# Queries first, keys last and two gate cells at the end of layer 1's first projections

## The chip, the core and the metric

The kernel runs on one core of a Trainium2 chip. Its engines are TensorE (PE in the profile; PEld is its weight load), VectorE (DVE), ScalarE (ACT), GpSimd (POOL) and SyncE (SP), each with an instruction queue of its own that it works off in order. Transfers between the chip's memory (HBM) and SBUF are issued on the queues of SP, ACT and POOL and carried by 16 DMA engines. The metric is the time of one execution on the device in microseconds (us): 3739.16 as the median of three runs, from 3738.85 to 3740.12.

## What is computed

Two layers of a diffusion backbone over 2048 latent tokens and 256 context tokens, width 1024, all in float32. Layer 0 is latent attention beside gated linear attention, layer 1 neighbourhood attention on a 32 by 64 grid. What matters here is the input projection of layer 1:

```
q, k, v, z = jnp.split(dot(h, w_in), 4, axis=-1)          # 16 heads of 64 each
q, k = rms_norm(heads(q), q_gain), rms_norm(heads(k), k_gain)
o = neighborhood_attention(q, k, v, k_ctx, v_ctx, rpb)
y = dot(o * silu(z), w_out)
```

Keys and values are wanted for all 2304 tokens, queries and the gate `z` for the latent ones only.

## The kernel before

Tokens lie in 18 row tiles of 128; tiles 0 and 1 are context. The columns of `w_in` lie in eight blocks of 512, numbered `j`: 0 and 1 queries, 2 and 3 keys, 4 and 5 values, 6 and 7 the gate. One **cell** (t, j) is the product of row tile t with column block j. Every float32 operand is split in a high and a low part, and the product is the sum of three (lines 129 to 131), so a cell is 24 matmuls of 128x512 into one PSUM bank (`gm`).

The projections stand in two functions. `odd_qk` runs the query and key cells and, at its end, the first two value cells (16, 4) and (17, 4). `odd_vz` runs the other value cells and the gate cells, from the last tile down, and weaves between them the scores `mx` whose block maxima (`maxes`) the attention needs later.

Only four column blocks of the weight have room at a time, in places `w0` to `w3`. Block 4 takes the place of block 2, 5 that of 3, 6 that of 0, 7 that of 1 (`OD_PLACE`). When the last cell of a block is issued, `done` hands its successor to `self.ahead`, and `pump` issues it piece by piece. A piece, here called a chunk, is 128x512 numbers, 256 KB: a load on SP (line 380, tile `wraw`, three in flight), ScalarE's copy as the high part and VectorE's difference as the low part (line 383). A load waits until the chunk three before it is split.

A query or key cell ends on ScalarE with squares (`osq`), on VectorE with sums (line 1135), on GpSimd with the power that makes the norm (lines 200 and 202), on VectorE with the scaled tile `onat` (line 1138). `fin` follows two cells later: four transposes into the bank `tp` (line 1146), then scaled copies. A query tile makes `oqh` and `oql`, stored to `Q1` by SP (line 1158). A key tile makes `oqh`, stored to `K1` by SP (line 1151), and its part of the grid-ordered `okt`; after every fourth latent tile `store_k` sends four stores of 512 KB to `K1t` on POOL (line 1179). A value cell only copies the bank (`onat` or `ovz`) and stores it to `V1` on POOL (line 1201). A gate cell takes a tanh on ScalarE, one product on VectorE (line 1227) that makes `z (1 + tanh(z/2))`, four transposes (line 1230), a copy `ozt` and a store to `z1` on ACT's queue (line 1234).

`cells` runs the first two and the last two tiles in pairs: before the change the last eight cells of `odd_qk`'s main list are keys (16, 2), (17, 2), (16, 3), (17, 3), then queries (16, 0), (17, 0), (16, 1), (17, 1).

The order in each engine's queue is not that of the source: a scheduler sets it when the kernel is built, by its own estimates of time. The pools of `odd_vz` take over the memory of `odd_qk`'s, and a tile of the new pool waits only for what lay in its bytes. VectorE clears the buffers `mz` (line 1239) and `mm` (line 1252) first, so it waits there for the stores that still read that memory. The loads of `mk` from `K1` (line 1246), of the bias table `mtab` (line 1248) and of `mq` from `Q1` (line 1258) wait on SP in the same way.

Of the kernel before, what the change touches and what calls it, by code (L numbers as in the profile page):

```python
# [10 lines left out]
F32 = mybir.dt.float32  # L11
F32R = mybir.dt.float32r
AF = mybir.ActivationFunctionType
ALU = mybir.AluOpType
# [3 lines left out]
P = 128  # L18
D = 1024
KD = D // P  # L20
SEQ = 2048
CTX = 256
T = SEQ + CTX
NT = T // P
NCT = CTX // P
# [63 lines left out]
class Kern:  # L89
# [1011 lines left out]
    def odd_qk(self, ws, win, hT):  # L1101
        nc = self.nc
        self.V1c = self.scr("V1c", (2, P, NCT, 512), F32)
        self.V1 = self.scr("V1", (2, SEQ, 512), F32)
        self.Q1 = self.scr("Q1", (2, 8, P, SEQ), F32)
        self.K1 = self.scr("K1", (8, P, T), F32)
        self.K1t = self.scr("K1t", (8, 2, P, T), F32)
        with ExitStack() as es:
            sp = self.pool(es, "osA", bufs=2, side="left", reuse_waits="tile")
            pp = self.pool(es, "opA", bufs=2, space=PSUM, reuse_waits="tile")  # L1110
            qkg = self.tl(sp, [P, 2], "oqkg", bufs=1)
            nc.sync.dma_start(qkg[:], self.i["od_gain"])
            nc.vector.tensor_scalar(out=qkg[:, 0:1], in0=qkg[:, 0:1], scalar1=0.125, scalar2=None, op0=ALU.mult)
            self.ahead += [self.od_steps(win, 0, ws), self.od_steps(win, 1, ws)]
            pend, kt = [], {}

            def cell(t, j):
                hi, lo = hT[t]
                wh, wl = win[j]
                ps = self.tl(pp, [P, 8, 64], "gm", bufs=3)  # L1120
                steps = self.mm3_steps(ps[:], (lambda k: hi[:, k, :], lambda k: lo[:, k, :]),
                                       (lambda k: wh[:, k, :], lambda k: wl[:, k, :]), range(KD))
                for n, _ in enumerate(steps):
                    if n == 5 and pend and (len(pend) > 1 or j == 4):
                        fin(*pend.pop(0))
                    yield
                if j == 4:
                    n = self.tl(sp, [P, 512], "onat", bufs=4)
                    self.act(n[:], ps[:].rearrange("p h d -> p (h d)"))
                    self.store_v(t, 0, n)  # L1130
                    return
                sq = self.tl(sp, [P, 512], "osq")
                self.act(sq[:], ps[:].rearrange("p h d -> p (h d)"), AF.Square)
                ss = self.tl(sp, [P, 8], "oss", bufs=4)
                nc.vector.tensor_reduce(out=ss[:], in_=sq[:].rearrange("p (h d) -> p h d", h=8), axis=AX.X, op=ALU.add)
                self.rpow(ss[:], ss[:], 1.0 / 64, EPS)
                n = self.tl(sp, [P, 512], "onat", bufs=4)
                nc.vector.tensor_tensor(out=n[:].rearrange("p (h d) -> p h d", h=8), in0=ps[:],
                                        in1=ss[:].unsqueeze(2).to_broadcast([P, 8, 64]), op=ALU.mult)
                pend.append((t, j, n))  # L1140

            def fin(t, j, n):
                z = j // 2
                ps = self.tl(pp, [P, 4, P], "tp")
                for i in range(4):
                    nc.tensor.transpose(ps[:, i, :], n[:, i * P : i * P + P], self.ident[:])
                hi = self.tl(sp, [P, 4, P], "oqh", F32R)
                self.act(hi[:], ps[:], AF.Copy, scale=qkg[:, z : z + 1])
                j0 = (j % 2) * 4
                if z == 1:  # L1150
                    nc.sync.dma_start(self.K1[j0 : j0 + 4, :, t * P : t * P + P].rearrange("j p t -> p j t"), hi[:].bitcast(F32))
                if z == 0 or t < NCT:
                    lo = self.tl(sp, [P, 4, P], "oql", F32R)
                    nc.vector.scalar_tensor_tensor(out=lo[:], in0=ps[:], scalar=qkg[:, z : z + 1], in1=hi[:],
                                                   op0=ALU.mult, op1=ALU.subtract)
                    if z == 0:
                        for part, tt in enumerate((hi, lo)):
                            nc.sync.dma_start(self.Q1[part][j0 : j0 + 4, :, (t - NCT) * P : (t - NCT) * P + P].rearrange("j p t -> p j t"),
                                              tt[:].bitcast(F32))
                    else:  # L1160
                        store_k((hi, lo), j0, t * P, P)
                    return
                g, r0 = divmod(2 * (t - NCT), 8)
                if r0 == 0:
                    kt[j] = [self.tl(sp, [P, 4, 512], f"okt{j}{part}", F32R, bufs=1) for part in range(2)]
                view = lambda x, n: x[:].rearrange("p i (r c b) -> p i r c b", r=n, c=4)
                for r in range(2):
                    oh, ol = (x[:].rearrange("p i (c b r) -> p i r c b", c=4, r=8)[:, :, r0 + r] for x in kt[j])
                    self.act(oh, view(ps, 2)[:, :, r], AF.Copy, scale=qkg[:, z : z + 1])
                    nc.vector.scalar_tensor_tensor(out=ol, in0=view(ps, 2)[:, :, r], scalar=qkg[:, z : z + 1],  # L1170
                                                   in1=view(hi, 2)[:, :, r], op0=ALU.mult, op1=ALU.subtract)
                if r0 == 6:
                    store_k(kt.pop(j), j0, CTX + g * 512, 512)

            def store_k(parts, j0, o, w):

                for u, x in enumerate(parts):
                    for i in range(2):
                        nc.gpsimd.dma_start(self.K1t[j0 : j0 + 4, i, u * 64 : u * 64 + 64, o : o + w].rearrange("j d t -> d j t"),
                                            x[i * 64 : i * 64 + 64].bitcast(F32))  # L1180

            nxt = {2: 4, 3: 5, 0: 6, 1: 7}
            done = lambda j: j in nxt and self.ahead.append(self.od_steps(win, nxt[j], ws))
            cells = self.cells(list(range(NT)), (2, 3, 0, 1), lambda t, j: j > 1 or t >= NCT) + [(NT - 2, 4), (NT - 1, 4)]
            for _ in self.stream(cells, hT, cell, lambda t: self.prep(1, t, self.x1, pp, ("px", 2)), done):
                self.pump()
            while pend:
                fin(*pend.pop(0))

    def by_tile(self, out, in_):  # L1190

        self.act(out.rearrange("d (c r b) -> d r c b", c=4, r=8), in_.rearrange("d (r c b) -> d r c b", r=8, c=4))
# [9 lines left out]

    def odd_vz(self, ws, win, hT):
        nc = self.nc
        self.z1 = self.scr("z1", (KD, P, SEQ), F32)
        self.M1 = self.scr("M1", (16, SEQ), F32)
        NR, NC = (len(b) for b in BLOCKS["q"])
        with ExitStack() as es:
# [6 lines left out]
            def cell(t, j):  # L1215
                hi, lo = hT[t]
                wh, wl = win[j]
                ps = self.tl(pp, [P, 512], "gm")
                yield from self.mm3_steps(ps[:], (lambda k: hi[:, k, :], lambda k: lo[:, k, :]),
                                          (lambda k: wh[:, k, :], lambda k: wl[:, k, :]), range(KD))  # L1220
                n = self.tl(sp, [P, 512], "ovz", bufs=3)
                if j < 6:
                    self.act(n[:], ps[:])
                    self.store_v(t, j - 4, n)
                    return
                self.last_tanh = self.act(n[:], ps[:], AF.Tanh, scale=0.5)
                nc.vector.scalar_tensor_tensor(out=n[:], in0=n[:], scalar=1.0, in1=ps[:], op0=ALU.add, op1=ALU.mult)
                pt = self.tl(pp, [P, 4, P], "tp", bufs=1)
                for i in range(4):
                    nc.tensor.transpose(pt[:, i, :], n[:, i * P : i * P + P], self.ident[:])  # L1230
                z = self.tl(sp, [P, 4, P], "ozt", bufs=1)
                self.act(z[:], pt[:])
                o = (t - NCT) * P
                nc.scalar.dma_start(self.z1[(j - 6) * 4 : (j - 6) * 4 + 4, :, o : o + P].rearrange("j p t -> p j t"), z[:])
# [53 lines left out]
                        nc.gpsimd.dma_start(self.M1[h, g * 512 : g * 512 + 512].rearrange("(a c b) -> c a b", a=8, c=4),  # L1288
                                            r[4 * g : 4 * g + 4].rearrange("c (a b) -> c a b", a=8).bitcast(F32))

            cells = self.cells(list(range(NT))[::-1], (4, 5, 6, 7), lambda t, j: (j > 4 or t < NT - 2) and (j < 6 or t >= NCT))
            gemms = self.stream(cells, hT, cell, lambda t: self.reload(1, t))
            self.weave(gemms, maxes(), 0.57, 15)

# [388 lines left out]
```

## Time and profile before

| | |
|---|---|
| median of three runs | 3739.16 us (3738.85 to 3740.12) |
| the profiled execution, whole | 3741.73 us |
| its span, first to last instruction | 3739.6 us |
| `odd_qk` about | 2188 to 2635 us |
| `odd_vz` about | 2635 to 3105 us |

A row of the timeline has the start in us, the duration, the engine, the source line, the operation and its tiles, output before `<-`; in brackets stands how long the engine had been idle before it and what released it. `x2` means that two equal instructions are merged. A line of the waits says who waited for whom, then the total, the count and the longest. In the table by stretches the columns are the stretch, its length, the busy time of PE, PEld, DVE, ACT and POOL with counts, the granted clock of TensorE, the mean busy share of the DMA engines and GB/s.

### The profile page before, as it was taken

How to read it: one execution, taken by the hardware profiler on the slowest of the kernel's cores; microseconds unless marked ns; L12 is line 12 of the kernel's file. 1: busy time of each engine (PE TensorE's matmuls, PEld its weight loads, DVE VectorE, ACT ScalarE, POOL GpSimd, SP SyncE). 2: the span in 40 equal slices, each digit the busy share in tenths (PEclk: the TensorE clock that was granted, in tenths of full speed). 3: DMA queues.
4: the chain of work that ended last, by engine and by line, in shares of the span. 5: the costliest groups of instructions: out<-in, count | busy, mean ns of one | idle time of the engine just before them, and what ended most of it. 6: DMA issues, size and time to landing. Idle time of an engine off the chain costs nothing.

```text
span 3739.6 us, 51736 instructions
## 1 busy us (share of the span) xinstructions
PE 3583.3 (96%) x18404; PEld 2768.3 (74%) x18404; DVE 2379.7 (64%) x4860; ACT 1437.7 (38%) x2741; POOL 1207.2 (32%) x1334
## 2 busy tenths in 40 slices
PE   8999989999999999999999999999899998898889
PEld 6988988888886666655657878887788885555567
DVE  4677656888866666697654344545678774666722
ACT  4445541111125555545552134444322223454400
POOL 1434330001011222212202233333344435776643
PEclk9999999999999999999999999999999998999899
DMA  7455462222252241434515545546544448777464
GB/s 254 137 165 160 128 172 94 84 75 86 74 137 66 69 114 56 115 88 137 142 51 169 165 148 149 146 142 182 183 141 143 130 116 223 186 182 201 141 194 132
DMA packets 365267, 512.18 MB, mean 137 GB/s; under 512 B 25825, under 2 KB 244913, under 8 KB 359106
## 3 DMA queue, kind: packets, MB, share of 16 engines
q1 hardware_dynamic: 322642, 425.49, 39.7%
q0 software_dynamic: 19712, 55.40, 4.9%
q10 hardware_dynamic: 22656, 27.99, 2.1%
q8 instruction: 146, 2.39, 0.3%
q14 instruction: 111, 0.91, 0.1%
HBM read 329.38 MB, written 179.37 MB: 136 GB/s over the span
## 4 chain that ended last, share of the span: by engine, by line
PE 79%; DVE 7%; DMA 6%; POOL 3%; ACT 3%; issue 2%; SPq 0%; POOLq 0%; DVEq 0%; ACTq 0%
PE gm L129 9%; PE gm L130 9%; PE gm L131 9%; PE av L905 7%; PE st L963 4%; PE mx L651 4%; PE st L964 3%; PE st L965 3%; PE pj L129 3%; PE pj L131 3%; PE pj L130 3%; DMA wraw<-w_od 2%; PE o L1393 2%; PE st L1363 2%; PE o L1375 1%
## 5 line engine op out<-in xcount | busy, mean ns | idle before, releaser
L954 DVE TENSOR_TENSOR acc<-acc,apt 128x512 f32<-128x512 f32 x512 | 364.5, 736 | 156.6 <-ACT apt L106 153.6
L106 ACT ACTIVATE apt<-st 128x512 f32<-128x512 f32 (+1 forms) x592 | 343.9, 593 | 283.9 <-PE st L965 246.5
L652 DVE TENSOR_REDUCE mm<-mx 128x1 f32<-128x512 f32 (+1 forms) x656 | 389.1, 628 | 82.2 <-PE mx L651 75.2
L905 PE MATMUL av<-apt,av 128*64 128x512 f32 (+1 forms) x1184 | 286.2, 597 | 0.0
L963 PE MATMUL st<-aq,akh 97*128 97x512 f32 (+1 forms) x592 | 254.1, 429 | 5.9 <-ACT apt L106 3.0
L1399 POOL TENSOR_TENSOR oacc<-oacc,opt 128x576 f32<-128x576 f32 (+6 forms) x192 | 221.4, 1179 | 86.6 <-ACT opt L106 84.9
L651 PE MATMUL mx<-mk,mq 96*128 96x512 f32 (+1 forms) x656 | 236.8, 373 | 5.8 <-DMA mq<-QT 4.6
L964 PE MATMUL st<-aq,akh 96*128 96x512 f32 (+1 forms) x592 | 235.1, 397 | 0.0
L965 PE MATMUL st<-aq,akl 96*128 96x512 f32 (+1 forms) x592 | 233.9, 396 | 0.0
L1277 DVE CUSTOM_DVE_ANT_1 mx<-mx,mtab 128x225 f32<-128x225 f32 (+13 forms) x576 | 183.6, 339 | 57.8 <-PE mx L1271 42.6
L106 ACT ACTIVATE u<-gm 128x352 f32<-128x352 f32 (+1 forms) x140 | 68.5, 497 | 369.5 <-PE gm L131 208.8
L905 PEld LDWEIGHTS av<-apt,av 128*64 128x64 f32 x1184 | 81.6, 137 | 155.4 <-issue 154.1
L1521 DVE TENSOR_TENSOR opt<-st,tab 128x64 f32<-128x64 f32 (+10 forms) x576 | 142.4, 315 | 79.9 <-PE st L1364 52.7
L963 PEld LDWEIGHTS st<-aq,akh 97*128 97x128 f32 x592 | 112.4, 190 | 99.0 <-issue 43.7
L1073 POOL TENSOR_TENSOR px<-py,px 128x512 f32<-128x512 f32 x64 | 86.3, 1349 | 234.3 <-DVE py L1072 223.0
L106 ACT ACTIVATE opt<-opt 128x930 f32<-128x930 f32 (+8 forms) x130 | 104.4, 805 | 138.9 <-DVE opt L1521 130.1
L1363 PE MATMUL st<-q,kt 128*128 128x480 f32 (+5 forms) x256 | 104.3, 409 | 47.7 <-DVE opt L1521 43.4
L651 PEld LDWEIGHTS mx<-mk,mq 96*128 96x128 f32 x656 | 121.7, 189 | 17.3 <-issue 5.0
L106 ACT ACTIVATE prh<-pr 128x1024 fp32r<-128x1024 f32 x32 | 33.8, 1057 | 261.6 <-PE pj L130 234.0
L965 PEld LDWEIGHTS st<-aq,akl 96*128 96x128 f32 x592 | 113.6, 192 | 25.6
L964 PEld LDWEIGHTS st<-aq,akh 96*128 96x128 f32 x592 | 114.1, 193 | 18.0
L129 PE MATMUL gm<-w1h,hhi 128*128 128x512 f32 x288 | 116.4, 404 | 6.0 <-ACT onat L106 6.0
(511 smaller groups left out, 10033.2 us busy)
## 6 DMA issues: line engine op xcount, KB each, us to landing
q<-Q SPq DMA_DIRECT2D x48, 512.0 KB
H<-x ACTq DMA_DIRECT2D x36, 512.0 KB
adaw<-ada_w SPq DMA_DIRECT2D x64, 256.0 KB
x<-H SPq DMA_DIRECT2D x32, 512.0 KB
pr<-RT SPq DMA_DIRECT2D x32, 512.0 KB
wraw<-w_od SPq DMA_DIRECT2D x64, 256.0 KB
K1t<-okt POOLq DMA_DIRECT2D x32, 512.0 KB, 7.4
kt<-K1t SPq DMA_DIRECT2D x32, 512.0 KB
```

The lines of the kernel that those rows point to most:

```text
L106: return self.nc.scalar.activation(out, in_, func, **kw)
L129: self.nc.tensor.matmul(out, lh(k), rh(k), start=j == 0, stop=False)
L130: self.nc.tensor.matmul(out, lh(k), rl(k), start=False, stop=False)
L131: yield self.nc.tensor.matmul(out, ll(k), rh(k), start=False, stop=j == n - 1)
L651: mm = nc.tensor.matmul(ps[:, :w], q[:A_QK, (t % 6) * P : (t % 6) * P + P], k[:A_QK, k0 : k0 + w], start=True, stop=True)
L652: nc.vector.tensor_reduce(out=m[:, t, n : n + 1], in_=ps[:, :w], axis=AX.X, op=ALU.max)
L905: nc.tensor.matmul(O[j, nb][i * 64 : i * 64 + 64, :w], V[j, kt // TT][:, kt % TT, i * 64 : i * 64 + 64], pts[i][:, :w], start=n == 0, stop ...
L954: nc.vector.tensor_tensor(out=acc[i][:, :w], in0=a[:, :w], in1=pts[i][:, :w], op=ALU.add)
L963: nc.tensor.matmul(ps[:, :w], kh[: A_QK + 1, i, kq], qh[: A_QK + 1, :w], start=True, stop=False)
L964: nc.tensor.matmul(ps[:, :w], kh[:A_QK, i, kq], ql[:A_QK, :w], start=False, stop=False)
L965: mm = nc.tensor.matmul(ps[:, :w], kl[:A_QK, i, kq], qh[:A_QK, :w], start=False, stop=True)
L1399: self.psum = nc.gpsimd.tensor_tensor(out=a, in0=a, in1=pts[:, :, a0 - r0 : a1 - r0, :], op=ALU.add)
```

## The change

The last eight cells of `odd_qk` become queries first, keys last, and the two cells at the end are the first half of the gate, block 6, in place of values. Since a block's successor is loaded when the block is through, weight 6 comes first, then 7, 4 and 5. The gate's tanh and product go into a helper, and in `odd_qk` the gate tile goes through `fin` like a query or key tile; its transposed copy takes an `oqh` buffer and is stored to `z1` on POOL's queue. `pend` is drained one by one in the cells of block 6; the two gate tiles themselves are finished after the last cell. `odd_vz` begins with the other gate half and then runs the values of tiles 17 and 16, (17, 7), (16, 7), (17, 4), (16, 4), (17, 5), (16, 5); before it began with (17, 5), (16, 5), (17, 6), (16, 6), (17, 7), (16, 7). From tile 15 down it is as before.

```diff
-                    if n == 5 and pend and (len(pend) > 1 or j == 4):
+                    if n == 5 and pend and (len(pend) > 1 or j == 6):
                         fin(*pend.pop(0))
                     yield
-                if j == 4:
+                if j == 6:
                     n = self.tl(sp, [P, 512], "onat", bufs=4)
-                    self.act(n[:], ps[:].rearrange("p h d -> p (h d)"))
-                    self.store_v(t, 0, n)
+                    self.gate(n, ps[:].rearrange("p h d -> p (h d)"))
+                    pend.append((t, j, n))
                     return
...
                 hi = self.tl(sp, [P, 4, P], "oqh", F32R)
+                if j == 6:
+                    self.act(hi[:].bitcast(F32), ps[:])
+                    nc.gpsimd.dma_start(self.z1[:4, :, (t - NCT) * P : (t - NCT) * P + P].rearrange("j p t -> p j t"), hi[:].bitcast(F32))
+                    return
...
-            cells = self.cells(list(range(NT)), (2, 3, 0, 1), lambda t, j: j > 1 or t >= NCT) + [(NT - 2, 4), (NT - 1, 4)]
+            cells = self.cells(list(range(NT)), (2, 3, 0, 1), lambda t, j: j > 1 or t >= NCT)[:-8]
+            cells += [(t, j) for j in (0, 1, 2, 3, 6) for t in (NT - 2, NT - 1)]
...
+    def gate(self, out, in_):
+
+        self.last_tanh = self.act(out[:], in_, AF.Tanh, scale=0.5)
+        self.nc.vector.scalar_tensor_tensor(out=out[:], in0=out[:], scalar=1.0, in1=in_, op0=ALU.add, op1=ALU.mult)
...
-            cells = self.cells(list(range(NT))[::-1], (4, 5, 6, 7), lambda t, j: (j > 4 or t < NT - 2) and (j < 6 or t >= NCT))
+            cells = [(t, j) for j in (7, 4, 5) for t in (NT - 1, NT - 2)]
+            cells += self.cells(list(range(NT))[::-1], (4, 5, 6, 7), lambda t, j: j < 6 or t >= NCT)[8:]
```

More of the change, by code (lines that the diff above doesn't have):

```diff
@@ L1105, in odd_qk @@
         self.Q1 = self.scr("Q1", (2, 8, P, SEQ), F32)
+        self.z1 = self.scr("z1", (KD, P, SEQ), F32)
         self.K1 = self.scr("K1", (8, P, T), F32)
@@ L1204, in odd_vz @@
         nc = self.nc
-        self.z1 = self.scr("z1", (KD, P, SEQ), F32)
         self.M1 = self.scr("M1", (16, SEQ), F32)
@@ L1225, in cell @@
                     return
-                self.last_tanh = self.act(n[:], ps[:], AF.Tanh, scale=0.5)
-                nc.vector.scalar_tensor_tensor(out=n[:], in0=n[:], scalar=1.0, in1=ps[:], op0=ALU.add, op1=ALU.mult)
+                self.gate(n, ps[:])
                 pt = self.tl(pp, [P, 4, P], "tp", bufs=1)
```

## The prediction

> **What bounds the kernel now.** The page first: TensorE is busy for 96% of the span, so a change counts only where it alters TensorE's idle time or its clock.
>
> ```profile
> span 3739.6 us, 51736 instructions
> PE 3583.3 (96%) x18404; PEld 2768.3 (74%) x18404; DVE 2379.7 (64%) x4860; ACT 1437.7 (38%) x2741; POOL 1207.2 (32%) x1334
> ```
>
> Then TensorE's waits between 2540 and 2720 us, where `odd_qk` hands over to `odd_vz` (total, times, longest), and its timeline there.
>
> ```profile
> PE gm L129 <- ACT onat L106: 6.0, 1, 6.0
> PE tp L1146 <- DVE onat L1138: 2.0, 1, 2.0
> PE tp L1230 <- DVE ovz L1227: 0.7, 2, 0.5
> ...
> 2582.85 0.60 ACT L106 ACTIVATE osq<-gm 128x512 f32<-128x512 f32 x1 [9.52 <-PE gm L131]
> 2613.05 0.40 PE L131 MATMUL gm<-w3h,hlo 128*128 128x512 f32 x1
> 2627.58 0.60 PE L1146 MATMUL tp<-ident,onat 128*128 128x128 f32 x4
> 2627.94 0.48 PE L129 MATMUL gm<-w0h,hhi 128*128 128x512 f32 x1
> 2629.17 0.40 PE L131 MATMUL gm<-w0h,hlo 128*128 128x512 f32 x1
> 2635.52 0.79 PE L129 MATMUL gm<-w1h,hhi 128*128 128x512 f32 x1 [5.95 <-ACT onat L106]
> 2639.43 0.39 PE L129 MATMUL gm<-w1h,hhi 128*128 128x512 f32 x1
> ```
>
> The reader is to see one place: the last value cell ends at 2629.5, and the first cell of `odd_vz` starts at 2635.5, because its PSUM bank is freed by ScalarE's copy of the last value tile. Why is that copy late? ScalarE runs its queue in order, and weight splits stand ahead of it.
>
> ```profile
> L106 ACT ACTIVATE w0h<-wraw x8: 622/632/662, 2583.3 to 2592.7; 128x512 fp32r<-128x512 f32 x8
> L106 ACT ACTIVATE w2h<-wraw x8: 629/632/635, 2617.3 to 2634.4; 128x512 fp32r<-128x512 f32 x8
> ...
> 2587.56 1.24 ACT L106 ACTIVATE w0h<-wraw 128x512 fp32r<-128x512 f32 x2
> 2593.22 0.77 ACT L106 ACTIVATE okt<-tp,oqkg 128x256 fp32r<-128x256 f32 x1
> 2594.40 0.63 ACT L106 ACTIVATE w1h<-wraw 128x512 fp32r<-128x512 f32 x1 [0.41 <-DMA wraw<-w_od]
> 2596.58 0.63 ACT L106 ACTIVATE w1h<-wraw 128x512 fp32r<-128x512 f32 x1 [1.55 <-DMA wraw<-w_od]
> 2605.85 0.67 ACT L106 ACTIVATE oqh<-tp,oqkg 128x512 fp32r<-128x512 f32 x1
> 2606.42 0.76 ACT L106 ACTIVATE okt<-tp,oqkg 128x256 fp32r<-128x256 f32 x1
> 2609.70 1.27 ACT L106 ACTIVATE w1h<-wraw 128x512 fp32r<-128x512 f32 x2 [0.97 <-DMA wraw<-w_od]
> 2625.14 1.28 ACT L106 ACTIVATE w2h<-wraw 128x512 fp32r<-128x512 f32 x2 [0.78 <-DMA wraw<-w_od]
> 2634.36 0.63 ACT L106 ACTIVATE w2h<-wraw 128x512 fp32r<-128x512 f32 x1 [0.53 <-DMA wraw<-w_od]
> 2634.89 0.58 ACT L106 ACTIVATE onat<-gm 128x512 f32<-128x512 f32 x1
> 2657.89 1.28 ACT L106 ACT_TABLE_LOAD   x1
> ```
>
> Four weights of eight 256 KB chunks each are replaced here, 32 chunks numbered in order: 4 and 5 at 2587.56, 8 at 2592.7, 9 at 2594.40, 10 at 2596.58, 14 and 15 at 2609.70, 19 and 20 at 2625.14, 24 at 2634.36. The last value copy stands right behind the 24th. The pace is 1.5 us a chunk (4th to 10th: 9.0 us for six) or 1.84 (19th to 24th: 9.2 for five) when only weights and small stores move, and far slower while the transposed keys (`K1t`, four 512 KB stores at a time) go out:
>
> ```profile
> 2594.36 0.67 POOL L1179 DMA_DIRECT2D K1t<-okt  x1
> 2609.03 1.30 POOL L1179 DMA_DIRECT2D K1t<-okt  x2 [8.09 <-ACT okt L106]
> 2611.17 1.25 POOL L1179 DMA_DIRECT2D K1t<-okt  x2
> ...
> DMA to landing us min/median/max: 4.6/7.4/11.1
> ...
> 2588.00:2592.00 4.00, 4.00 (x21) 3.30 (x20) 3.41 (x7) 2.94 (x6) 1.83 (x2) 1.00 0.65 217
> 2600.00:2604.00 4.00, 4.00 (x21) 3.35 (x20) 2.11 (x4) 1.31 (x2) 0.93 (x1) 1.00 1.02 343
> ```
>
> From the first burst's start at 2594.36 the fifth chunk after the 9th comes 15.3 us later (14th), from the second's at 2609.03 the fifth after the 14th 16.1 us later (19th). The DMA share (next to last column) goes from 0.65 to 1.02. So weights, not arithmetic, time the handover.
>
> **The change part by part.** The eight cells of row tiles 16 and 17 keep their number and their matmuls (24 each, 0.23 us apart). Reordering them alone removes nothing. Weight 6 now takes query 0's place, 7 query 1's, 4 and 5 the keys': the same positions in the stream, so each weight is still needed as many cells after its load as before; nothing.
>
> Queries first: eight Q1 stores on SP move ahead of the four K1 stores, so the chunks between are held by query stores, two a cell, instead of key stores, one a cell. I take 1.7 us a chunk, between the two paces above; 1.5 and 1.84 are the ends. From the 8th at 2592.7, the 24th comes at 2592.7 + 16 x 1.7 = 2619.9, 14 us earlier than now, since no K1t burst has yet begun.
>
> Keys last: the first K1t burst now waits for the last key tile's copies, which stand behind the 24th chunk. It starts at about 2621.7 (a row-square and the copy, then 1.1 us as from 2593.22 to 2594.36). Ahead of TensorE's next work now stand more chunks. In the built order the tanh of gate cell 16 follows the 28th chunk, that of cell 17 the 29th; the transposes of the last two gate tiles, and before them those of the last key tile, stand on TensorE ahead of the first matmul of `odd_vz`; and the last group needs a bank that ScalarE empties after the 30th chunk, one `oqh`, one `okt` and one gate copy. The 25th is about due when the burst begins, as the 9th and 14th were; the 30th, five later, comes 15.3 to 16.1 us after it by those rows, 8.5 without slowing. I take 15.0, near the first burst, whose stores were keys too: 2636.7. Then 0.55 + 0.57 + 0.6 + 0.7 on ScalarE (the starts from 2605.85 on are 0.57 apart) and one transpose group at half clock, 0.75: TensorE restarts at 2639.9 against 2635.5. **+4.4 us** (ends -2.2 and +5.5). The end of its last cell is no cover: from 2582.85, with four matmuls and five cells to go, the row at 2613.05 closes the sixth; two more end at 2624.7.
>
> The table load for tanh moves ahead of the gates. It stands between the 28th and 29th chunk, hidden by the wait for the latter; uncovered it would cost its 1.28 us.
>
> The z1 stores go from ACT's queue to POOL's, among the second K1t burst: z1, four K1t, z1. `odd_vz` reuses the buffers that they read. VectorE's clearing of `mz` and `mm` must wait until both z1 stores and the last K1t have landed; now it waits for the value stores (2641.67 below), with only weight splits behind. In the new order the product of the first gate cell of `odd_vz` stands behind it, and TensorE's transposes behind that.
>
> ```profile
> 2641.67 1.02 DVE L1239 MEMSET mz<- 64x512 f32 x2 [0.16 <-issue]
> 2642.85 1.03 DVE L1239 MEMSET mz<- 64x512 f32 x2 [0.16 <-DVE mz L1239]
> 2644.39 0.22 DVE L1252 MEMSET mm<- 128x80 f32 x2
> 2660.24 0.67 DVE L1227 SCALAR_TENSOR_TENSOR ovz<-ovz,gm 128x512 f32<-128x512 f32 x1
> ```
>
> The second burst starts at 2640.7 (31st chunk, then the second `okt` copy, whose start is 2.9 us after the 30th's, and 1.1). Now its like lands 2611.8 + 11.1 - 2609.0 = 13.9 us after its first issue; so 2654.6. Clearing and product, 1.0 + 0.2 + 0.6: 2656.4. TensorE wants the transposes 48 matmuls after its restart, 11.0 us and 1.9 for the nine at half clock (3.91 us from 2635.52 to 2639.43): 2652.8. **+3.6 us**; ends 0 (landing in 4.6) and 5. A wait of 2.0 us at 2613 cost six slow matmuls, so **+1.2 us** for the clock.
>
> By the Trainium skill, page "TensorE: Matmul & The Clock Gate", "What's actually happening", the clock halves after an idle window of some 3.4 us and returns after as much work. A whole such window would make this term 1.7 and the sum 8.3; the trace has slow matmuls after 2.0 us already, so the row is kept.
>
> Gone from `odd_vz`: two groups of four transposes, 0.36 us each (2627.58 to 2627.94), **-0.7**, and the 0.7 that its first gates waited, **-0.7**. Two value cells come in, whose stores on POOL stand among the mask additions; nothing, while TensorE does not wait for maxima (below). The two gates' own transposes in `odd_qk` are in the 4.4.
>
> Sum: 4.4 + 3.6 + 1.2 - 0.7 - 0.7 = **+7.8 us**, on a span of 3739.6. That execution took 3741.73 in all, 2.6 above the median of the runs; the change is added to the median: 3739.16 + 7.8 = 3747.0.
>
> **The rivals.** *Only the first wait.* The second burst lands before TensorE comes: +3.0, 3742.2. For it speaks the shortest landing, 4.6 us; against it the 11.1 of a burst beside other loads, with the next part's key load beside it now as the weights were then.
>
> By the Trainium skill, page "DMA: Bandwidth & Descriptors", "Anatomy of one DMA", a transfer takes 2.0 us and its bytes at 436 GB/s; four K1t stores in a row would be down after an estimated 6.8 us, and this rival would hold. The trace's median of 7.4 for one disagrees.
>
> *Not slower: the burst does not slow the weights.* Place: chunks 25 to 30. At 1.7 each the 30th comes at 2630.1, the restart at 2633.3, and no landing is late: -2.2 - 1.4 = -3.6, 3735.6. It decides when the 30th is split before 2632.3. Against it stand both bursts' rows.
>
> *The old wait goes and nothing replaces it:* all 30 chunks are there at 2624.7; restart at 2628.0, -7.5 - 1.4 = -8.9, 3730.3. It needs 1.0 us a chunk from the 8th on, which no stretch shows.
>
> *A third wait.* The bias table is loaded only once K1t has left the buffer it takes, and its additions on POOL alternate with value stores.
>
> ```profile
> 2643.07 0.33 SPq L1248 DMA_DIRECT2D mtab<-rpb_q  x1
> 2653.08 3.20 POOL L1249 TENSOR_TENSOR mtab<-mtab,maskq 128x1798 f32<-128x1798 f32 x1 [2.55 <-DMA mtab<-rpb_q]
> 2659.73 8.24 POOL L1250 TENSOR_TENSOR mtab<-mtab,maskq 128x1798 f32<-128x1798 f32 x2
> ...
> L1277 DVE CUSTOM_DVE_ANT_1 mx<-mx,mtab 128x225 f32<-128x225 f32 (+13 forms) x576 | 183.6, 339 | 57.8 <-PE mx L1271 42.6
> ```
>
> Issued at 2654.6 in the worst case, 10.0 us to the first addition, additions of 3.2, 3.2 and 4.1 and seven maxima of 0.34: 2677.5. TensorE comes to the first block that needs their banks 63 matmuls, eleven small ones (about 2 us) and two transpose groups after 2656.4, with 1.2 for the clock: 2675.0. So 2.5 and 1.2 for the clock: +11.5, 3750.7. With a landing in 7.4 us the table is there in time; so I count nothing in the sum.
>
> **How the numbers follow.** Chances: forecast 0.55, only the first wait 0.16, not slower 0.10, nothing replaces it 0.05, third wait 0.14. The forecast's own range is 3743 to 3752. What a measurement of this kernel tells from no change is 0.2%, 7.5 us: slower above 3746.6. Some two thirds of the forecast's chance and the third wait lie there, 0.50; below 3731.7 lies 0.05; the rest is 0.45. The range, 3737.5 to 3753, leaves out the fifth case and the ends of the third and the last.
>
> **What would show it.** The 24th chunk split near 2620 and the 30th near 2637; TensorE idle from 2625 to 2640, released by ScalarE or VectorE through `onat` or `oqh`; one K1t burst at 2622, one at 2641; `mz` cleared near 2655 and TensorE waiting for `ovz` some 13 us after its restart. Wrong it would be if the weights keep their pace through the burst, or if the gate's product runs before the clearing.

## The result and the profile after

The changed kernel takes 3751.43 us (median of 8 runs, 3747.89 to 3754.97), the kernel before 3743.07 in the runs beside it (8 runs, 3738.85 to 3747.41). The ratio is 1.0023, with a 95% interval of 1.0013 to 1.0034: 8.4 us slower, where 7.8 were forecast. A second set of runs gave 3745.16 (11 runs) against 3738.20 (33 runs), a ratio of 1.0016, 1.0007 to 1.0025. Both intervals leave out 1, so the sign is sure. The two estimates of the size are 6 and 9 us, and their intervals together reach from 3 to 13.

The profiled execution took 3753.82 us in all. Its page begins so (span; then busy time, share of the span and instructions of each engine):

```profile
span 3751.7 us, 51747 instructions
...
PE 3587.1 (96%) x18404; PEld 2772.4 (74%) x18404; DVE 2375.7 (63%) x4860; ACT 1437.8 (38%) x2741; POOL 1206.8 (32%) x1336
```

TensorE has the same matmuls and the same share as before; the page alone shows no change. TensorE's waits between 2540 and 2740 us do (total, times, longest):

```profile
PE tp L1147 <- DVE onat L1139: 6.3, 2, 4.5
PE tp L1147 <- ACT oqh L106: 5.4, 1, 5.4
...
PE tp L1239 <- DVE ovz L1199: 2.4, 1, 2.4
...
PE mx L1280 <- DVE mm L1275: 0.8, 1, 0.8
PE mx L1280 <- DVE mm L1286: 0.5, 1, 0.5
```

The wait of 6.0 us for the value copy is gone. In its place stand 4.5 and 5.4 us at the transposes ahead of `odd_vz`, and 2.4 at the first gate of `odd_vz`. The timeline tells what is late (ScalarE's row square that opens the region; then, engine by engine, chunks 24 and 30; the two bursts; the clears; TensorE):

```profile
2585.85 0.60 ACT L106 ACTIVATE osq<-gm 128x512 f32<-128x512 f32 x1 [9.52 <-PE gm L131]
...
2624.24 0.63 ACT L106 ACTIVATE w0h<-wraw 128x512 fp32r<-128x512 f32 x1 [1.18 <-DMA wraw<-w_od]
2633.62 1.28 ACT L106 ACT_TABLE_LOAD   x1
2640.53 0.63 ACT L106 ACTIVATE w1h<-wraw 128x512 fp32r<-128x512 f32 x1 [4.02 <-DMA wraw<-w_od]
...
2626.30 0.67 POOL L1184 DMA_DIRECT2D K1t<-okt  x1 [6.99 <-ACT okt L106]
2630.42 1.66 POOL L202 TENSOR_TENSOR oss<-oss,mhalf 128x8 f32<-128x8 f32 x1
2643.07 0.81 POOL L1151 DMA_DIRECT2D z<-oqh  x1 [10.99 <-ACT oqh L106]
2644.21 2.48 POOL L1184 DMA_DIRECT2D K1t<-okt  x4 [0.33 <-ACT okt L106]
2646.68 0.76 POOL L1151 DMA_DIRECT2D z<-oqh  x1
...
2634.15 0.68 DVE L1139 TENSOR_TENSOR onat<-gm,oss 128x512 f32<-128x512 f32 x1
2650.21 0.48 DVE L1248 MEMSET mz<- 64x512 f32 x1 [4.42 <-DMA z<-oqh]
2657.24 1.03 DVE L1248 MEMSET mz<- 64x512 f32 x2 [6.54 <-DMA z<-oqh]
2658.37 1.21 DVE L1199 SCALAR_TENSOR_TENSOR ovz<-ovz,gm 128x512 f32<-128x512 f32 x2
...
2634.98 1.09 PE L1147 MATMUL tp<-ident,onat 128*128 128x128 f32 x4 [4.54 <-DVE onat L1139]
2642.83 1.12 PE L1147 MATMUL tp<-ident,onat 128*128 128x128 f32 x4 [5.42 <-ACT oqh L106]
2643.60 0.78 PE L129 MATMUL gm<-w3h,hhi 128*128 128x512 f32 x1
2659.05 0.66 PE L1239 MATMUL tp<-ident,ovz 128*128 128x128 f32 x4 [2.42 <-DVE ovz L1199]
```

The region opens 3.0 us later than in the profile of before (2585.85 against 2582.85). Nothing that was changed lies ahead of that, so it is scatter between two executions, and times are counted from this row square on. The 24th chunk is split 38.4 us after it (before: 51.5) and the 30th 54.7. TensorE restarts after 57.7 us, where it restarted after 52.7. The last cell of `odd_vz` begins its last matmul after 532.7, where it was 523.1: +9.6 us in this pair, +7.7 with the second profile of the changed kernel.

### The profile page after: what moved, and what is told of

The parts are those of the page before. It is cut to its first block, busy times and chain, and to the rows that moved or that the text cites. A ratio compares the mean times of both kernels' runs of the same rounds, so it can differ in the third digit from the quotient of the medians.

```text
span 3751.7 us, 51747 instructions
## 1 busy us (share of the span) xinstructions
PE 3587.1 (96%) x18404; PEld 2772.4 (74%) x18404; DVE 2375.7 (63%) x4860; ACT 1437.8 (38%) x2741; POOL 1206.8 (32%) x1336
## 4 chain that ended last, share of the span: by engine, by line
PE 78%; DVE 8%; DMA 6%; POOL 4%; ACT 3%; issue 2%; SPq 0%; POOLq 0%; DVEq 0%; ACTq 0%
PE gm L129 9%; PE gm L130 9%; PE gm L131 9%; PE av L905 7%; PE st L963 4%; PE mx L651 4%; PE st L964 3%; PE st L965 3%; PE pj L129 3%; PE pj L130 3%; PE pj L131 3%; POOL oacc L1409 2%; PE o L1403 1%; DMA wraw<-w_od 1%; PE st L1373 1%
## 5 line engine op out<-in xcount | busy, mean ns | idle before, releaser
L1286 DVE CUSTOM_DVE_ANT_1 mx<-mx,mtab 128x225 f32<-128x225 f32 (+12 forms) x576 | 183.8, 339 | 61.4 <-PE mx L1280 45.9
L106 ACT ACTIVATE x<-px,modB,modA 128x128 f32<-128x128 f32 x272 | 99.1, 468 | 57.9 <-DVE onat L1139 27.6
```

Source lines behind the costliest of these rows:

```text
L106: return self.nc.scalar.activation(out, in_, func, **kw)
```

## The experiments

The theory before them: the two bursts of K1t stores, moved to the handover, slow the weights that time TensorE's restart, and the traffic of the second one holds VectorE's clears, with a gate's product and TensorE's transposes behind them. The main rival: the weights are slow for other reasons, and the order costs nothing.

This table sums up all runs. Times are in us from the region's first row square (for a kernel with the stages moved, the matching one), worked out from each profile as in the paragraph above; the last column is the last matmul of `odd_vz`. "Restart" is the first matmul of `odd_vz`, "ovz wait" what TensorE waits for `ovz` at the first gates there.

| kernel | ratio to before (95%) | chunk 24 | chunk 30 | restart | ovz wait | end of `odd_vz` |
|---|---|---|---|---|---|---|
| before | 1 | 51.5 | 61.4 | 52.7 | 0.7 | 523.1 |
| changed | 1.0023 (1.0013 to 1.0034) | 38.4 | 54.7 | 57.7 | 2.4 | 532.7 |
| changed_again | 1.0016 (1.0007 to 1.0025) | 37.1 | 54.0 | 57.0 | 3.2 | 530.8 |
| no_last_bursts | 1.0039 (1.0026 to 1.0051) | 37.3 | 46.8 | 53.3 | 0 | 519.8 |
| clears_on_gpsimd | 1.0007 (0.9996 to 1.0018) | 37.4 | 55.0 | 58.1 | 0 | 526.3 |
| order_only | 1.0049 (1.0037 to 1.0062) | 36.4 | 53.6 | 45.8 | 10.4 | 540.4 |
| no_pair_old_order | 1.0049 (1.0036 to 1.0061) | 50.7 | 80.4 | 44.2 | 0.6 | 541.3 |
| gate_store_on_act | 1.0017 (1.0008 to 1.0026) | 37.2 | 54.0 | 57.0 | 2.3 | 528.0 |
| old_order_no_last_bursts | 1.0022 (1.0013 to 1.0031) | 35.1 | 45.0 | 51.3 | 0 | 518.4 |
| old_order_other_banks | 1.0001 (0.9992 to 1.0010) | 53.8 | 62.7 | 46.8 | 0 | 523.2 |
| second_burst_doubled | 1.0039 (1.0024 to 1.0053) | 37.8 | 54.7 | 57.8 | 10.2 | 537.3 |
| four_buffers_old_order | 0.9985 (0.9976 to 0.9993) | 47.8 | 55.6 | 54.7 | 0 | 521.3 |
| four_buffers_new_order | 0.9991 (0.9982 to 1.0000) | 29.3 | 38.7 | 50.7 | 4.1 | 524.6 |
| four_buffers_and_clears | 0.9976 (0.9968 to 0.9985) | 30.0 | 39.4 | 51.5 | 0 | 520.7 |

The run changed_again is the changed kernel a second time, on the chip of some of the others: 6 to 11 us over the kernel before, a restart at 57 to 59 and an ovz wait of 2 to 3 were expected, and 6 to 7 us, 57.0 and 3.2 came.

### Do the bursts slow the weights?

```diff
+            for j in (2, 3):
+                zero = self.tl(sp, [P, 4, 512], f"okt{j}0", F32R, bufs=1)
+                nc.vector.memset(zero[:].bitcast(F32), 0.0)
...
+                nc.gpsimd.dma_start(self.K1[j0 : j0 + 4, :, CTX + 1536 : CTX + 2048].rearrange("j p t -> p j t"), zero[:].bitcast(F32))
...
-                if r0 == 6:
+                if r0 == 6 and (g < 3 or j not in (2, 3)):
                     store_k(kt.pop(j), j0, CTX + g * 512, 512)
```

> The changed kernel without its last two K1t bursts: at the start of the part, zeros are stored as the last quarter of the latent keys of both key weights (in K1t and in K1), K1 stores of the real tiles go to a spare place of the same size, and the last two bursts of four 512 KB are left out. So part of the result is computed from zero keys; every instruction from 2590 us on is the same but those eight stores. Theory (the bursts slow the weights, and their landing holds the clears): chunks 25 to 30 come at 1.7 us each, the 30th about 7 us earlier against the region's first row square (45 us after it in place of 54.7), TensorE's restart some 6 us earlier, its wait for ovz (2.4) goes; in all 7 to 10 us under the changed kernel: 3742 to 3745, no slower than the kernel before. The ten stores at the start may cost up to 3 us there, before the region. Rival (weights are slow for another reason, the small stores or ScalarE's own queue): 30th chunk and restart stay within 1.5 us, at most the 2.4 goes: 3749 to 3752.

The 30th chunk comes 46.8 us after the row square, 7 to 8 us earlier than in the two profiles of the changed kernel (54.7, 54.0), while the 24th is where it was. That is the theory's size: the bursts slow the six chunks that they meet. The restart gains less, 4 us, because in this kernel's built order the last tanh stands behind the 32nd chunk. From the row square to the end of `odd_vz` it is 11 to 13 us shorter than the changed kernel. The whole is not faster, though: with the ten stores of zeros at the start the row square comes at 2594.92, 9 and 14 us later than in the two profiles of the changed kernel, where up to 3 were expected. Between 2100 and 2240 us TensorE waits 14.5 us here, against 4.4 and 2.7 in those two. The ovz wait is gone too, but that proves less: this kernel's clears wait for no store, since other tiles lie in that memory.

> The kernel before without its last two K1t bursts, made as in no_last_bursts: zeros stored at the start of the part as the last quarter of the latent keys of both key weights, the real tiles' K1 stores to a spare place, so part of the result is computed from zero keys. Theory (the same bursts time the old handover too): the 24th chunk comes some 14 us earlier after the first row square (37 in place of 51.5), the wait of 6.0 us at the bank goes altogether, and from that row square to the last matmul of odd_vz it is 6 to 8 us shorter than in the kernel before; the start costs 6 to 9 us before that, as it did in no_last_bursts. Rival (the old wait comes of the copy's place in ScalarE's queue, whatever the weights' pace): the wait stays over 3 us.

The same edit in the old order brings the 24th chunk 16 us forward, to 35.1. The wait does not go; it grows to 7.8 us. ScalarE's queue says why:

```profile
2627.00 0.62 ACT L106 ACTIVATE w2h<-wraw 128x512 fp32r<-128x512 f32 x1
...
2641.51 0.63 ACT L106 ACTIVATE w3h<-wraw 128x512 fp32r<-128x512 f32 x1 [1.84 <-DMA wraw<-w_od]
2642.62 0.59 ACT L106 ACTIVATE onat<-gm 128x512 f32<-128x512 f32 x1
```

In this kernel's built order the last value copy stands behind the 32nd chunk instead of the 24th. So the rival's number held here: it is the copy's place in the queue that makes the wait, and the weights' pace decides what that place costs. The theory's 6 to 8 us from there to the end of `odd_vz` came to 4.7.

### Does the second burst hold the clears?

```diff
-                    nc.vector.memset(z[64 - i * 64 : 128 - i * 64].bitcast(F32), 0.0)
+                    nc.gpsimd.memset(z[64 - i * 64 : 128 - i * 64].bitcast(F32), 0.0)
-                    nc.vector.memset(m[:], -3e38)
+                    nc.gpsimd.memset(m[:], -3e38)
```

> The changed kernel with the clears of mz and mm in odd_vz on GpSimd in place of VectorE; nothing is left out. Theory (the gate's product stands behind clears that wait for landings): TensorE's wait for ovz of 2.4 us goes, and the slow matmuls after it; restart unchanged at 2643.6: 2.4 to 3.5 us under the changed kernel, 3748 to 3749. Rival (the wait only moves: the clears hold up the mask additions on GpSimd, and TensorE waits for the first maxima instead): ovz wait gone, but 2 us or more at the first blocks of maxima, time within 1 us of the changed kernel.

In its timeline GpSimd now does the waiting, and TensorE's transposes of the first gate run without a wait, ahead of the clears:

```profile
2653.95 0.98 POOL L1248 MEMSET mz<- 64x512 f32 x2 [6.28 <-DMA z<-oqh]
2654.89 0.27 POOL L1261 MEMSET mm<- 128x80 f32 x2
...
2652.76 0.60 PE L1239 MATMUL tp<-ident,ovz 128*128 128x128 f32 x4
```

The restart stays (58.1). The time falls to within 0.07% of the kernel before, where the changed kernel was 0.16 to 0.23% above it: 3 to 6 us, as the theory said or a little more. The intervals overlap, but the profile agrees: `odd_vz` ends 4 to 6 us earlier (526.3 against 530.8 and 532.7). The first maxima wait as in the changed kernel (0.8 and 0.5 us), so nothing took its place.

```diff
-                    store_k(kt.pop(j), j0, CTX + g * 512, 512)
+                    store_k(kt[j], j0, CTX + g * 512, 512)
+                    if g == 3 and j in (3,):
+                        store_k(kt[j], j0, CTX + g * 512, 512, self.K1x)
+                    kt.pop(j)
...
```

> The changed kernel with the second of the last K1t bursts (keys of weight 3) stored a second time, to a spare place: eight 512 KB stores in a row in place of four; nothing is left out, and each engine's work up to them is in the same order. Theory (VectorE's clears stand for the landing of the traffic that begins here, the gate's product and TensorE's transposes behind them): restart unchanged at 57 to 58 us after the first row square, the ovz wait of 2.4 to 3.2 us grows by 8 to 12, the time by 8 to 12 over the changed kernel (some 1.004 of the kernel before). Rival (the clears wait for the small z1 stores only, one of which goes out ahead of the burst): ovz wait under 5, time within 3 us of the changed kernel.

TensorE's wait at the first gate, and VectorE's timeline, of this kernel:

```profile
PE tp L1243 <- DVE ovz L1203: 10.2, 1, 10.2
```

```profile
2643.35 0.48 DVE L1252 MEMSET mz<- 64x512 f32 x1 [4.10 <-DMA z<-oqh]
2659.11 1.03 DVE L1252 MEMSET mz<- 64x512 f32 x2 [15.27 <-issue]
2660.24 1.21 DVE L1203 SCALAR_TENSOR_TENSOR ovz<-ovz,gm 128x512 f32<-128x512 f32 x2
```

The restart is unmoved (57.8), the wait grows by 7 to 8 us, a little under the 8 to 12 expected, and the time stands at 1.0039, some 6 to 9 us over the changed kernel. Nothing but the traffic of the second burst was altered, so that traffic decides when the clears may run; the product follows them at once. What releases them is the second z1 store, issued behind the eight and landed at 2658.90, so the rival's condition (z1 alone) is not excluded by this run, only its number.

```diff
-                    nc.gpsimd.dma_start(self.z1[:4, ...
+                    nc.scalar.dma_start(self.z1[:4, ...
```

> The changed kernel with the two z1 stores of the last pair on ScalarE's queue in place of GpSimd's, where the second of them stands behind four K1t stores; nothing is left out. It tells which landing holds VectorE's clears. If it is that of z1 (the clears of mz wait for it): ovz wait of 2.4 goes or falls under 1, 2 to 4 us under the changed kernel beside it. If it is that of the K1t burst (the clears of mm wait for it): ovz wait unchanged, time within 1 us of the changed kernel.

Which landing is it? The two z1 stores are now issued on a queue of their own (the first row, a view by tile, has their first and last start), and the clears still wait for them (the timeline behind it):

```profile
L1151 ACTq DMA_DIRECT2D z<-oqh x2: 377/389/401, 2643.1 to 2645.7; - x2
```

```profile
2650.94 0.48 DVE L1248 MEMSET mz<- 64x512 f32 x1 [4.79 <-DMA z<-oqh]
2657.11 1.03 DVE L1248 MEMSET mz<- 64x512 f32 x2 [5.68 <-DMA z<-oqh]
```

Wait and time are those of the changed kernel (2.3 us; 1.0017 against 1.0016 beside it). By the expectation that points at K1t, while the timeline names z1. The time can't tell them apart: in the changed kernel the last K1t store landed at 2656.25 and the second z1 store at 2656.92, 0.7 us apart. What the run does show is that the place behind four K1t stores on GpSimd's queue is not what makes z1 late: on a queue of its own it takes 7.8 and 11.4 us from the issue to the clear that it releases. Not all of that is the burst's. In no_last_bursts, with no K1t store near and the next part's loads keeping the DMA engines busy (share 0.98 from 2648 to 2657), the two z1 stores landed after 7.4 and 7.7 us; in the changed kernel it was 7.0 and 10.2. Only the second is longer beside the burst, by some 2.5 us.

### Order or pair?

```diff
-            cells += [(t, j) for j in (0, 1, 2, 3, 6) for t in (NT - 2, NT - 1)]
+            cells += [(t, j) for j in (0, 1, 2, 3) for t in (NT - 2, NT - 1)]
-            cells = [(t, j) for j in (7, 4, 5) for t in (NT - 1, NT - 2)]
+            cells = [(t, j) for j in (6, 7, 4, 5) for t in (NT - 1, NT - 2)]
```

> The changed kernel's order of the eight query and key cells (queries first, keys last) without the extra pair of gate cells at the end; odd_vz then starts with its four gate cells of these tiles. Nothing is left out. Theory (keys last move the bursts to the handover; the pair fills the gap that this opens): TensorE stops 11 us earlier, restarts near 2632 (behind the split of chunk 27), and then waits for the first gate's product behind the clears, which wait for the second burst's landing near 2652: some 7 us more than in the changed kernel in that wait, in all 4 to 8 us over the changed kernel, 3755 to 3760. Rival (the order costs nothing, the gate pair does): 3739 to 3743, as the kernel before.

> The kernel before without its extra pair of value cells at the end of odd_qk: keys first, queries last, then odd_vz starts with the four value cells. Nothing is left out. Theory (weights time the handover; with queries last no burst is in the way of its end): TensorE needs no bank that a late copy frees until its third cell, so the wait moves by two cells and shrinks or stays: 3737 to 3742. Against order_only this gives the price of the order alone: 12 us or more by the theory, under 3 by the rival that the order costs nothing.

The second kernel takes the two value cells out of the old order in the same way. TensorE's waits of order_only, a row of VectorE's timeline there, and TensorE's waits of no_pair_old_order:

```profile
PE tp L1147 <- DVE onat L1139: 13.4, 2, 9.3
PE tp L1239 <- DVE ovz L1199: 10.4, 1, 10.4
```

```profile
2649.77 0.22 DVE L1261 MEMSET mm<- 128x80 f32 x2 [8.53 <-DMA K1t<-okt]
```

```profile
PE tp L1146 <- DVE onat L1138: 11.1, 3, 5.0
PE mx L1271 <- DVE mm L1277: 8.6, 1, 8.6
```

For order_only the theory held in mechanism (here the clears wait for K1t itself) and, with 1.0049, in size. But no_pair_old_order stands at 1.0049 as well, where 3737 to 3742 us were expected. The theory's price for the order alone, 12 us or more, falls: without an extra pair of cells both orders cost the same, each to within 5 us, and the rival is right there. What differs is the worth of the pair. Two value cells in the old order save 18 us (1.0049 to 1); two gate cells in the new one save 10 to 12 (1.0049 to 1.0023 or 1.0016), worked out from the ratios on some 3740 us. A likely reason is that a value cell needs only a copy of its bank, while the gate cells bring a tanh, a product, two groups of transposes and their copies ahead of the restart, beside the K1t bursts. This is argued, not shown: no kernel put a value pair behind the new order, so what is due to the gate and what to the order around it stays open.

### Can the wait be taken out?

```diff
+            mx = self.pool(es, "opM", bufs=5, space=PSUM, reuse_waits="tile")
...
```

The line stands ahead of the pool `opB`, and the three `mx` tiles are then taken from it.

> The kernel before with odd_vz's banks for the maxima reserved ahead of those of its cells (a pool of their own), so that its first two cells use banks that have long been free and the last value's copy releases none of them. Queues are in the same order; nothing is left out. Theory (the wait of 6.0 us is for that bank alone, and its third cell's banks come free some 11 us later): the 6.0 goes, at most 1.5 comes back at the third cell: 4 to 6 us under the kernel before, the fastest of all. Rival (weights and maxima are late anyway): what is saved at the handover comes back at the third cell and at the first maxima, and the time is within 1 us of the kernel before.

TensorE's waits in that kernel:

```profile
PE gm L129 <- ACT ovz L106: 4.6, 1, 4.6
...
PE mx L1265 <- ACT mz L106: 2.2, 1, 2.2
```

The wait for the bank goes (`odd_vz` starts at 46.8 in place of 52.7), and it comes back two cells later: the copies of the first two `odd_vz` cells stand behind the same chunks. Ratio 1.0001. The rival holds: a free bank buys nothing while the weights are late.

```diff
-            self.prep_pool(e1, "prp1", "left", 2, 3)
+            self.prep_pool(e1, "prp1", "left", 2, 4)
...
```

The last number is that of the `wraw` buffers; the lines left out take `onat` from four buffers to three and `ovz` from three to two.

> The kernel before with four staging buffers for weight chunks in place of three; to make room, onat has three buffers in place of four in odd_qk and ovz two in place of three in odd_vz. Nothing is left out. Theory (weights time the handover, and each chunk waits for a buffer that is in flight, under conversion or under subtraction): the pace falls from 1.5 to 1.6 us a chunk towards 1.2 where no burst runs, the 24th chunk comes 4 to 8 us earlier, the 6.0 us wait shrinks to 0 to 3: 2 to 5 us under the kernel before. Rival (the bursts fill the DMA engines, a further buffer only waits there): 24th chunk within 2 us, time within 2 us or above it for the buffers taken away.

> The changed kernel with the same four staging buffers (onat three, ovz two). Theory: chunks 9 to 24, which run without a burst here, come at 1.2 to 1.3 us in place of 1.7, and the 30th 4 to 8 us earlier; restart 50 to 54 us after the first row square in place of 57 to 58; 3 to 7 us under the changed kernel, about level with the kernel before. Rival (as beside it): 30th chunk within 2 us, time within 2 us of the changed kernel.

Chunks 9, 24 and 30 on ScalarE, first of changed_again, then of four_buffers_new_order:

```profile
2593.64 0.63 ACT L106 ACTIVATE w3h<-wraw 128x512 fp32r<-128x512 f32 x1 [2.12 <-DMA wraw<-w_od]
...
2617.96 0.63 ACT L106 ACTIVATE w0h<-wraw 128x512 fp32r<-128x512 f32 x1 [1.09 <-DMA wraw<-w_od]
...
2634.86 0.63 ACT L106 ACTIVATE w1h<-wraw 128x512 fp32r<-128x512 f32 x1 [4.49 <-DMA wraw<-w_od]
```

```profile
2591.28 1.95 ACT L106 ACTIVATE w3h<-wraw 128x512 fp32r<-128x512 f32 x3 [0.19 <-DMA wraw<-w_od]
...
2610.56 0.66 ACT L106 ACTIVATE w0h<-wraw 128x512 fp32r<-128x512 f32 x1
...
2619.97 0.65 ACT L106 ACTIVATE w1h<-wraw 128x512 fp32r<-128x512 f32 x1
...
2630.57 0.60 ACT L106 ACTIVATE oqh<-tp 128x512 f32<-128x512 f32 x1 [2.80 <-DMA K<-oqh]
```

From the 9th to the 24th chunk it was 24.32 us for fifteen, 1.62 each; with four buffers 19.28, 1.29 each. The tables by stretches show the DMA engines the busier for it (share 0.74 and 0.94):

```profile
2594.00:2618.00 24.00, 23.38 (x111) 19.05 (x110) 16.32 (x26) 14.31 (x26) 6.20 (x6) 1.00 0.74 224
```

```profile
2591.00:2610.00 19.00, 19.00 (x91) 15.67 (x90) 15.52 (x26) 12.93 (x23) 5.40 (x5) 1.00 0.94 290
```

The 30th comes 15 us earlier, more than expected, since most of the six now run ahead of the burst. The restart gains 6 to 7 us and no more: now the last copy into `oqh` waits until a K1 store has left that buffer. The time is 9 to 12 us under the changed kernel by the ratios, more than the 3 to 7 expected and than the 6 to 8 that `odd_vz` ends earlier.

In the old order the 24th chunk comes 3.7 us earlier and the wait at the bank shrinks as expected, but a longer wait has come ahead of it. TensorE's waits of four_buffers_old_order, and VectorE's timeline:

```profile
PE tp L1146 <- DVE onat L1138: 9.0, 1, 9.0
PE gm L129 <- ACT onat L106: 0.7, 1, 0.7
```

```profile
2623.72 0.69 DVE L383 TENSOR_TENSOR w2l<-wraw,w2h 128x512 fp32r<-128x512 f32 x1 [4.79 <-ACT w2h L106]
2624.33 1.28 DVE L1138 TENSOR_TENSOR onat<-gm,oss 128x512 f32<-128x512 f32 x2
```

Here `onat` stands in VectorE's queue behind the difference of a late chunk, and TensorE waits 9.0 us for it, where the kernel before waited 2.0. So weights still time this handover, by another path, and the restart is 2 us later (54.7 against 52.7). `odd_vz` ends only 1.8 us earlier, so where the 5.6 us of this kernel's ratio come from is not shown by its profile. Both orders end under the kernel before, at 0.9985 and 0.9991.

> The changed kernel with both remedies: four staging buffers for weight chunks (onat three, ovz two) and the clears of mz and mm on GpSimd. Nothing is left out. Theory (the two waits are separate terms that add): restart 50 to 51 us after the first row square as in four_buffers_new_order, the ovz wait of 4.1 us there gone, 3 to 6 us under that kernel: 0.9975 to 0.9985 of the kernel before, level with four_buffers_old_order or faster. Rival (the terms cover one another: a later bound, the bias table and the maxima, takes what is saved): within 1.5 us of four_buffers_new_order, 0.9988 to 0.9995.

With both remedies the changed order takes 3731.92 us (12 runs) against 3738.91 (17 runs): 0.9976, the lowest ratio of all, though its interval overlaps that of four_buffers_old_order. That is 0.15% under four_buffers_new_order, 5.6 us, for an ovz wait of 4.1 us that is gone; in the profiles `odd_vz` ends 3.9 us earlier. So the two waits are separate terms that add.

## Why the prediction was right, step by step

**What bounds the kernel.** That weights time the handover is shown: in the new order one more staging buffer brings the restart 6 to 7 us forward, while in the old order a free bank only moves the wait on by two cells. What the prediction left out is that the built order moves with the edits: in old_order_no_last_bursts and in four_buffers_old_order the weights come sooner, and another copy or tile then stands behind them.

**First wait, forecast +4.4, restart at 2639.9.** Less the 3.0 us of scatter, the 24th chunk came at 2621.2 (forecast 2619.9), the first burst began at 2623.3 (2621.7), the 30th chunk was split at 2637.5 (2636.7), and TensorE restarted at 2640.6. That is +5.1 (57.75 against 52.67), and +4.4 in the second profile. The 15.0 us for five chunks past the burst's start held (14.2), though it was taken below both rows it came from (15.3 and 16.1), and no_last_bursts shows the cause. One thing had no step: nearly half of the idle time, 4.5 us, is for the last key tile's `onat`. GpSimd's power for its norm is at 2630.42, behind the four issues of the burst, and VectorE comes to `onat` at 2634.15. As the 30th chunk was later still, it need not have cost anything by itself; no run takes it out.

**Second wait, forecast +3.6 and +1.2 for the clock.** The mechanism is shown by clears_on_gpsimd and second_burst_doubled. The landing was right: the last `mz` clears begin at 2654.2 less scatter, forecast 2654.6. The working had put the longest landing of the first burst, 11.1 us, on the last store of the second, which landed after 10.8, so its 13.9 should have been 13.6. The wait was 2.4 us in the first profile, where TensorE came 0.8 us later than forecast, and 3.2 in the second, not 3.6. From the start of the 48th matmul after the restart to that of the 72nd the kernel before took 5.5 us and the changed kernel 8.6 and 11.0, worked out from the starts in the trace: +3.1 and +5.5 for wait, transposes and clock together, where 4.8 was forecast. The clock makes most of that difference. After the wait of 2.4 us the matmuls go on 0.23 us apart, so the 1.2 was nothing there; after 3.2 us nine of them run at the slow pace, 0.43 us apart, some 1.6 us in all. That a wait of 2.0 us cost six slow matmuls in the kernel before was no rule.

**Credits, forecast -0.7 and -0.7.** From the 72nd matmul to the 120th the changed kernel won back 0.9 us in both profiles (15.4 against 16.3), not 1.4.

**What was counted at nothing.** The first maxima wait 0.8 and 0.5 us where the kernel before waited 0.6; the third wait did not come. Of the reordering alone the prediction said that it removes nothing, and order_only beside no_pair_old_order agrees in the time, 1.0049 each, with other waits in each.

**The sum.** Up to the 120th matmul it is 5.1 + 3.1 - 0.9 = 7.3 us in the first profile and 4.4 + 5.5 - 0.9 = 9.0 in the second, forecast 7.8. At the end of `odd_vz` it is 9.6 and 7.7. What comes between, +2.3 and -1.3, has no common cause: TensorE's waits for `mc` after 2740 us are alike in both (5.0 and 4.9 us, 3.6 before), and the two profiles of one kernel lie 1.9 us apart at the end. So 7.8 was right in mechanism and in size, and its single terms hold to about 2 us; that the sum came closer than its terms is in part luck.

**The rivals.** The one with only the first wait needed a quick landing of the second burst; the z1 stores beside it were issued at 2643.07 and 2646.68, and the clears behind them began at 2650.21 and 2657.24, 7.1 and 10.6 us later. By the Trainium skill, page "DMA: Bandwidth & Descriptors", section "Anatomy of one DMA", a store of 256 KB issued on GpSimd is down after an estimated 2.6 us; the trace disagrees. The case in which nothing replaces the old wait was put on too hard a condition: from the 8th chunk at 2592.7 to the 30th at 2624.7 are 32.0 us for 22 chunks, 1.45 each and not 1.0. The three buffers still did not reach it (1.62 and then the burst), but four did: in four_buffers_new_order the 30th chunk comes 38.7 us after the row square, where 2624.7 is 41.9 after that of the kernel before. TensorE still restarted only after 50.7, behind the K1 store named above.

## What to carry to other kernels

When cells are moved around a handover, follow the transfers that they issue: here the stores that came last delayed the weights, the clears of the next part and, through an in-order queue, a product that needs neither. A filler is worth the idle time that it covers less the work that it puts ahead of the restart; here two value cells in one order were worth some 18 us and two gate cells in the other 10 to 12. Before moving waits about, try the resource behind them: in the changed order a fourth staging buffer and clears on an engine that has time took out what other banks and another queue only moved.

## What was not expected of the hardware

Outside the bursts the weights' pace was set by the three staging buffers, not by the DMA engines: 1.62 us a chunk at a DMA share of 0.74 became 1.29 with four, at 0.94. A store of 256 KB took 7.8 and 11.4 us from its issue to the clear that it released while four of 512 KB ran on another queue, so a queue of its own did not shield the small transfer; without those four, among loads, it still took 7.4 and 7.7. Ten large stores at the start of a part went with 10 to 12 us more of TensorE's waits there, where up to 3 were expected. And the same kind of wait did not always slow TensorE's clock: six slow matmuls after 2.0 us (before), none after 2.4 (changed) and 2.3 (gate_store_on_act), nine after 3.2 (changed_again).
